# Splitting the low halves of weights and mixed values into pieces of 256 columns on GpSimd

## The chip, the cores and the metric

The kernel runs on one core of a Trainium2 chip. The metric is the device time of one execution, in microseconds (us). Several engines work side by side on a core: TensorE (PE; its weight loads are shown apart as PEld), VectorE (DVE), ScalarE (ACT), GpSimd (POOL) and SyncE (SP, which here issues the DMAs). Each works through its own queue in the order in which the program was written, and waits for the others by semaphores.

## The reference

It is a decoder of two layers over 512 positions with a width of 1024, all in 32-bit floats. In each layer a normed stream is projected once, and five groups of four heads read that projection; the groups' outputs are concatenated and projected back, and a gated MLP with a short causal convolution follows.

```
for l in range(DEPTH):                       # 2 layers
    xn = _rms_norm(x, attn_norm[l])
    h = xn @ w_in[l]
    ...                                      # per group: norm, rotary, softmax attention
    o_a = _dense_causal_attention(q_a, k_a, v_a, ...)          # "mla", low-rank q, k, v
    o_b = _dense_causal_attention(q_b, k_b, v_b, ..., decay)   # "fox", with a forgetting bias
    o_c = _moba_attention(q_c, k_c, v_c, ...)                  # "moba"
    o_d = _diff_causal_attention(q1, q2, k1, k2, v_d, lam, ...)  # "diff", two softmaxes
    o_d = _rms_norm(o_d, diff_sub_norm[l]) * (1.0 - lam_init)
    o_e = _memory_attention(q_e, k_e, v_e, ...)                # "mem", over 256 memory rows
    mixed = jnp.concatenate([_merge(o) for o in (o_a, o_b, o_c, o_d, o_e)], axis=-1)
    x = x + mixed @ w_o[l]
    xn = _rms_norm(x, ffn_norm[l])
    gate = _causal_dwconv(xn @ ffn_w_gate[l], ffn_conv_w[l], ffn_conv_b[l])
    x = x + (jax.nn.silu(gate) * (xn @ ffn_w_up[l])) @ ffn_w_down[l]
```

## The kernel before

**Products in two halves.** To keep the precision of 32-bit products, an operand is split into a high half h (a rounded copy, written as the type fp32r) and a low half l = value - h. A product of two such operands is three matmuls: h by h, h by l and l by h. Splitting is work of the other engines: for each weight ScalarE writes the high half (L419) and a subtraction gives the low half (L421). The same pair of operations splits the mixed values, the outputs of an attention pair, ahead of the output projection: L874 and L876 for most groups, L912 and L914 for the differential group. In the MLP the gated activation is split in L1625 and L1627.

**Weights.** An object of the class `Weight` stands for one load of up to 768 columns by 128 rows. It takes a staging buffer `ws` (there are 2), SP issues the load, then it takes one of 6 buffers `wh` and one of 6 `wl`, ScalarE and the subtraction fill them, and `ws` goes free for the next load. Matmuls that use a weight are planned after its `loaded` event. A layer's weights have 768, 712, 512 or 256 columns.

**The order of the work.** The kernel's code is a set of tasks, written as Python generators, and a planner in the file (`Flow`) lets them run against an estimated clock. A task yields either an event, a buffer that it needs, or a request for an engine with an estimated duration; requests that can go to one of several engines are a tuple of offers. When the planner starts an operation, the instruction is issued, so that the order in each engine's queue is the order that the planner found. An offer's estimated end is the start plus a weighted duration plus an extra:

```
    def begin(self, f, port=False):
        t = max(self.engine[f], self.now)
        return max(t, self.port) if port or f == "P" else t

    def finish(self, f, c, extra=0.0, port=False):

        return self.begin(f, port) + c * self.WEIGHT[f] + extra
```

The weights are 1.5 for VectorE ("V") and 0.6 for GpSimd ("P"). The estimate for n columns on VectorE is `both(n)` = 68 + 1.04 n ns, and on GpSimd `gps(n)` = 150 + 2.1 n ns; `vp(n)` offers both. `port` models a port that GpSimd's operations and those of VectorE marked True use one at a time. For a weight, VectorE's offer has an extra of `dear`, 400 ns, or 0 for the first layer's first weights.

**The stages.** A layer's attention part goes through the five groups in pairs of heads, in an order written out by hand (`ORDER`): projection, head norms and rotary (`rope`, L633 to L635; `rstd`, L502 and L504), scores (L763, L795), softmax (`soft`, L641 and L646), in the differential group the combination of two softmaxes (L801, L803) and the splitting of its heads (L334, L1429, with transposes in L1437), transposes (L653), the product with the values (L847, L855), and the mixed values. Output projections are accumulated into x by L974. The MLP then runs in two halves of 11 blocks of 128 columns: `ff` (L1603 to L1627) and `down` (L1675, L1696).

Of the kernel before, what the change touches and what calls it, by code (L numbers as in the profile page):

```python
# [13 lines left out]
OP = mybir.AluOpType  # L14
# [14 lines left out]
NPAIR = 2  # L29
HALF_F = NF // 2  # L30
BLK = 6

# [28 lines left out]
def mm4(n):  # L63
    return "T", 4 + max(214.0, 1.667 * n)
# [7 lines left out]
def tr(n):  # L72
    return "T", 109.0 * n - 70.0


def vec(n):
    return "V", 68 + 1.04 * n
# [11 lines left out]
def act(n):  # L89
    return "A", 94 + 0.833 * n  # L90


def both(n):

    return "V", 68 + 1.04 * n, 0.0, True


def gps(n):
    return "P", 150 + 2.1 * n
# [10 lines left out]
def dma(nbytes):  # L110
    return "D", nbytes / 330.0
# [20 lines left out]
class Flow:  # L132
# [39 lines left out]
    def free(self, tag, n=1):  # L172
        for _ in range(n):
            self.at(max(self.now, self.cur.end) + 60.0, self.freed, tag)
# [118 lines left out]
def trunk(ctx: ExitStack, tc: tile.TileContext, x_in, mem, pos, norms, sm, lam, cols, conv,  # L293
          win_mla, win_pair, win_mem, mkv, uq, ukv, w_o, gu, w_down, out):
    nc = tc.nc
    V, A, P, T = nc.vector, nc.scalar, nc.gpsimd, nc.tensor
    ENG = {"V": V, "P": P}
# [11 lines left out]
    def sbt(shape, tag, dtype=F32):  # L309
        return sb.tile(shape, dtype, name=tag + "_t", tag=tag, bufs=SLOTS[tag])  # L310

    def bank(tag):
        return ps.tile([128, 512], F32, name=tag + "_p", tag=tag, bufs=SLOTS[tag])

    def f32(ap):
        return ap.bitcast(F32)
# [4 lines left out]
    def tables(name):  # L321
        if loaded_set[0] != name:
            loaded_set[0] = name
            A.preload_act_table_set(name)
            S_.engine["A"] += 1283.0
            S_.cur.end += 1283.0
# [12 lines left out]
    def vp(n):  # L339
        return (both(n), gps(n))  # L340
# [57 lines left out]
    class Weight:  # L398
# [6 lines left out]
        def load(self):  # L405
            n = self.n
            yield self.tks[0]
            stg = sbt([128, 768], "ws")
            dst = stg[:, :n]
            if len(self.shape) == 2:  # L410
                dst = dst.rearrange("p (a b) -> p a b", a=self.shape[0])
            yield dma(512 * n)
            nc.sync.dma_start(dst, self.src)
            yield self.tks[1]
            yield self.tks[2]
            self.h = sbt([128, 768], "wh", F32R)
            self.l = sbt([128, 768], "wl", F32R)
            yield act(n)
            A.activation(self.h[:, :n], stg[:, :n], AF.Copy)  # L419
            e = yield (("V", 68 + 1.04 * n, self.dear, True), gps(n))  # L420
            ENG[e].tensor_tensor(out=self.l[:, :n], in0=stg[:, :n], in1=f32(self.h[:, :n]), op=OP.subtract)  # L421
            free("ws")

        def done(self):
# [235 lines left out]
    class Pair:  # L660
# [156 lines left out]
        def close(self, heads):  # L817
            kind, p = self.kind, self.p
            yield heads[0]
            yield heads[1]  # L820
            yield self.mx.open
            yield "V", 75.0, 0.0, True
            V.reciprocal(self.su[:, 8:16], self.su[:, 0:8])
            yield "e"
            o = sbt([128, 512], "e")
            yield act(512)
            A.activation(o.rearrange("p (k d) -> p k d", d=64), self.su[:, 8:16, None].to_broadcast([128, 8, 64]),
                         AF.Copy)
            free("st", 2 if kind == "diff" else 1)
            yield "tp"  # L830
            tp = bank("tp")
            yield tr(4)
            for i in range(NT):
                T.transpose(tp[:, 128 * i:128 * i + 128], o[:, 128 * i:128 * i + 128], ident)  # L834
            yield act(512)
            A.activation(o, tp, AF.Copy)
            free("tp")
            yield "o"
            ob = bank("o")

            for j in range(2 if kind == "mem" else NT):
                n = 512 if kind == "mem" else 512 - 128 * j
                yield "T", 4 + max(214.0, 1.667 * n) + 20
                for a in range(2):
                    pt, h = self.pt[a], slice(64 * a, 64 * a + 64)
                    if kind == "mem":
                        T.matmul(ob[h, :], self.extra.vt[:, 2 * p + j, h], pt[:, :, 128 * j:128 * j + 128],  # L847
                                 start=j == 0, stop=j == 1)
                    else:
                        if j == 3:  # L850
                            mv = pt[:, 1536:1664]
                        else:
                            mv = pt[:, 384 * j:1536].rearrange("p (i c) -> p i c", c=384)
                            mv = mv[:, :, 128 * j:128 * j + 128]
                        T.matmul(ob[h, 128 * j:512], self.src.vt[:, j, h], mv, start=j == 0, stop=j == 3)  # L855
            free("pt", 2)
            self.src.uses -= 1
            if not self.src.uses:
                if kind == "mem":
                    free("kt")  # L860
                    free("v")
                    free("qk")
                else:
                    free("v")
                    free("qk", len(self.src.qk))
            yield vec(512)
            V.tensor_tensor(out=o, in0=ob, in1=o, op=OP.mult)
            free("o")
            if kind == "diff":
                yield from self.sub_norm(o)  # L870
                return
            dst = self.mx.tile[:, p]
            yield act(512)
            A.activation(dst[:, 0, :], o, AF.Copy)  # L874
            e = yield vp(512)
            ENG[e].tensor_tensor(out=dst[:, 1, :], in0=o, in1=f32(dst[:, 0, :]), op=OP.subtract)  # L876
            free("e")

        def sub_norm(self, o):
            yield self.tk_n  # L880
            w = sbt([128, 3, 512], "pt")
            sq, y, t = w[:, 0, :], w[:, 1, :], w[:, 2, :]
            yield "A", 52 + 0.833 * 512
            A.activation(sq, o, AF.Square)
            yield "s"
            sm_ = bank("s")
            yield mm4(512)
            T.matmul(sm_, blk, sq, start=True, stop=True)
            yield "V", 65 + 1.04 * 512
            V.tensor_scalar(sq, sm_, 1.0 / 64, EPS, op0=OP.mult, op1=OP.add)  # L890
            free("s")
            yield "A", 520.0
            tables(EXP_LN)
            A.activation(y, sq, AF.Ln)
            yield "A", 520.0
            tables(EXP_LN)
            A.activation(y, y, AF.Exp, scale=-0.5)
            g = yield (("A", 52 + 0.833 * 512), both(512))
            if g == "A":
                A.activation(t, y, AF.Square)  # L900
            else:
                V.tensor_tensor(out=t, in0=y, in1=y, op=OP.mult)
            yield "V", 130 + 1.04 * 512, 0.0, True
            V.scalar_tensor_tensor(t, t, -0.5, sq, op0=OP.mult, op1=OP.mult)
            yield "V", 130 + 1.04 * 512, 0.0, True
            V.scalar_tensor_tensor(y, t, 1.5, y, op0=OP.add, op1=OP.mult)
            yield "V", 130 + 1.04 * 512, 0.0, True
            V.scalar_tensor_tensor(t, o, self.extra.sg, y, op0=OP.mult, op1=OP.mult)
            free("e")
            dst = self.mx.tile[:, self.p]  # L910
            yield act(512)
            A.activation(dst[:, 0, :], t, AF.Copy)  # L912
            e = yield vp(512)
            ENG[e].tensor_tensor(out=dst[:, 1, :], in0=t, in1=f32(dst[:, 0, :]), op=OP.subtract)  # L914
            free("pt")


# [195 lines left out]
    def layer(l, normed, rms, wm, Ly, memkv, rot):  # L1113
# [433 lines left out]
        per = HALF_F * 16  # L1547
        nt = -(-per // BLK)

        def gu_block(f, i):  # L1550
            hf, b = divmod(16 * f + i, per)
            ti, bi = divmod(b, BLK)
            if (hf, ti) not in gtiles:
                n = min(BLK, per - BLK * ti)
                gtiles[hf, ti] = Weight(gu[l, hf * nt + ti, :, :n * 128], [n * 128], n)
# [166 lines left out]
    for item in "x0 w0 x1 w1 w2 w3 x2 x3".split():  # L1722
        t = int(item[1])
# [17 lines left out]
def layout(inp):  # L1741
# [45 lines left out]
    per = HALF_F * 16  # L1787
    nt = -(-per // BLK)
    gu = np.stack([g["ffn_w_gate"], g["ffn_w_up"]], axis=1)
    gu = gu.reshape(L, 2, KD, 128, NF, 128).transpose(0, 4, 1, 2, 3, 5).reshape(L, 2, per, 128, 128)  # L1790
    pad = np.zeros((L, 2, nt * BLK, 128, 128), np.float32)
    pad[:, :, :per] = gu
    a["gu"] = c(pad.reshape(L, 2 * nt, BLK, 128, 128).transpose(0, 1, 3, 2, 4).reshape(L, 2 * nt, 128, BLK * 128))
    a["w_down"] = c(g["ffn_w_down"])
# [24 lines left out]
```

## Time and profile before

| | |
|---|---|
| median of 3 runs | 1454.44 us (1454.09 to 1459.37) |
| profiled execution | 1452.53 us, of which the span from first to last instruction is 1450.8 us |
| TensorE busy | 1386.6 us (96%), granted clock 0.982 |
| VectorE busy | 802.0 us (55%) |
| ScalarE busy | 758.4 us (52%) |
| GpSimd busy | 605.1 us (42%) |
| DMA | 117.46 MB, 81 GB/s over the span |

In the profile a row of a group of instructions gives the line, engine and operation, the tiles written and read, the shapes and the count, then the busy time in us and the mean duration in ns, then the engine's idle time ahead of them and what ended it. A row of the chain gives the start, the length and the instruction; a row of a timeline the start, the length, the engine, the line and the operation. A row of the waits says who waited for whom, for how long in total, how often, and the longest time. Busy time is an average over stages: the attention parts stand at about 50 to 400 us and 750 to 1100 us, the MLP of the first layer at 400 to 745 us, that of the second from 1100 us to the end.

### The profile page before, as it was taken

The page shows a single profiled execution, that of the slowest core. Times are in us where ns is not written, and L with a number is a line of the kernel's source. Part 1 is how long each engine was busy: PE and PEld are TensorE (multiplying, and loading weights), DVE is VectorE, ACT ScalarE, POOL GpSimd, SP SyncE. Part 2 cuts the span into 40 slices and gives each one's busy share as a digit, 9 for nine tenths or more (in the row PEclk, how much of TensorE's full clock was granted, in tenths as well). Part 3 has the DMA queues.
Part 4 walks back from the last instruction along what each step waited for, and adds up shares of the span by engine and source line. Part 5 has one row for each costly group of instructions (what it writes and reads, how often), then busy time and mean ns, then how long its engine had stood idle before and what let it go on. Part 6 is the DMA issues. An engine that isn't in the chain of part 4 may idle for free.

```text
span 1450.8 us, 21241 instructions
## 1 busy us (share of the span) xinstructions
PE 1386.6 (96%) x7392; PEld 1172.5 (81%) x7392; DVE 802.0 (55%) x2073; ACT 758.4 (52%) x1968; POOL 605.1 (42%) x423
## 2 busy tenths in 40 slices
PE   6899989999999999999999999999989999999998
PEld 5788777876888888888888887888669888888887
DVE  7777789665654402544057877887654541145411
ACT  8678566766733322433266876756764332233321
POOL 3422133333655445654532223323244554465542
PEclk9899999999999999999999999999999999999999
DMA  5311122212333233332231211220122322343223
GB/s 179 105 47 36 30 69 67 63 55 86 117 104 95 71 98 109 115 98 71 90 103 44 56 30 49 67 75 30 59 89 79 97 81 79 102 131 98 76 80 109
DMA packets 51530, 117.46 MB, mean 81 GB/s; under 512 B 6496, under 2 KB 7648, under 8 KB 51424
## 3 DMA queue, kind: packets, MB, share of 16 engines
q1 hardware_dynamic: 51424, 116.11, 26.4%
q8 instruction: 58, 0.95, 0.3%
q14 instruction: 48, 0.39, 0.1%
HBM read 113.99 MB, written 2.10 MB: 80 GB/s over the span
## 4 chain that ended last, share of the span: by engine, by line
PE 86%; DVE 7%; ACT 4%; issue 1%; DMA 0%; POOL 0%; DVEq 0%; SPq 0%; POOLq 0%; ACTq 0%
PE acc_p L479 32%; PE s_p L479 9%; PE o_p L479 8%; PE tp_p L479 8%; PE acc_p L1675 6%; PE tp_p L1675 4%; PE s_p L1675 4%; PE tp_p L653 3%; PE o_p L855 2%; PE o_p L1675 2%; PE s_p L763 2%; PE tp_p L513 1%; PE tp_p L1437 1%; DVE e_t L803 1%; PE tp_p L834 1%
## 5 line engine op out<-in xcount | busy, mean ns | idle before, releaser
L421 POOL TENSOR_TENSOR wl_t<-ws_t,wh_t 128x768 fp32r<-128x768 f32 (+3 forms) x322 | 517.2, 1612 | 624.7 <-ACT wh_t L419 568.1
L419 ACT ACTIVATE wh_t<-ws_t 128x768 fp32r<-128x768 f32 (+3 forms) x322 | 240.5, 750 | 408.2 <-DMA ws_t<-in_w_down_dram 73.2
L479 PE MATMUL acc_p<-wh_t,xh 128*128 128x384 f32 (+2 forms) x512 | 184.7, 361 | 0.4 <-DVE qn_t L933 0.4
L479 PE MATMUL acc_p<-wh_t,xl 128*128 128x384 f32 (+2 forms) x512 | 170.2, 332 | 0.0
L479 PE MATMUL acc_p<-wl_t,xh 128*128 128x384 f32 (+2 forms) x512 | 170.0, 332 | 0.0
L1608 DVE SCALAR_TENSOR_TENSOR e_t<-e_t,convt 128x511 f32<-128x511 f32 x44 | 67.6, 1536 | 172.1 <-ACT e_t L1606 172.1
L479 PE MATMUL acc_p<-wh_t,mx_t 128*128 128x512 f32 x320 | 118.6, 423 | 4.9 <-DVE x L974 2.7
L646 ACT ACTIVATE e_t<-e_t,st_t 128x256 f32<-128x256 f32 (+3 forms) x192 | 104.9, 548 | 30.0 <-DVE st_t L641 29.1
L479 PEld LDWEIGHTS acc_p<-wh_t,xh 128*128 128x128 f32 x512 | 99.0, 193 | 4.2 <-issue 1.9
L479 PEld LDWEIGHTS acc_p<-wl_t,xh 128*128 128x128 f32 x512 | 98.9, 193 | 1.0 <-issue 0.2
L479 PEld LDWEIGHTS acc_p<-wh_t,xl 128*128 128x128 f32 x512 | 98.3, 192 | 0.0
L641 DVE CUSTOM_DVE_ANT_0 e_t<-s_p,mask 128x256 f32<-128x256 f32 (+3 forms) x160 | 72.8, 473 | 23.3 <-PE s_p L763 10.0
L1618 DVE TENSOR_TENSOR e_t<-e_t 128x512 f32<-128x512 f32 x44 | 67.0, 1522 | 26.8 <-ACT e_t L1613 25.4
L479 PEld LDWEIGHTS acc_p<-wh_t,mx_t 128*128 128x128 f32 x320 | 63.5, 199 | 20.0 <-DVE x L974 3.3
L332 ACT ACTIVATE pt_t<-tp_p 128x256 f32<-128x256 f32 (+3 forms) x137 | 58.0, 432 | 35.4 <-PE tp_p L653 33.6
L653 PE MATMUL tp_p<-identr,e_t 128*128 128x128 f32 x384 | 68.2, 279 | 8.4 <-DVE e_t L803 7.7
L479 PE MATMUL acc_p<-xh,wh_t 128*128 128x512 f32 (+1 forms) x192 | 72.1, 375 | 0.0
L479 PE MATMUL acc_p<-xl,wh_t 128*128 128x512 f32 (+1 forms) x192 | 71.5, 372 | 0.0
L479 PE MATMUL s_p<-xh,wh_t 128*128 128x512 f32 (+1 forms) x192 | 71.4, 372 | 0.0
L479 PE MATMUL acc_p<-xh,wl_t 128*128 128x512 f32 (+1 forms) x192 | 71.4, 372 | 0.0
L479 PE MATMUL o_p<-xh,wh_t 128*128 128x512 f32 (+1 forms) x192 | 71.3, 371 | 0.0
L479 PE MATMUL o_p<-xl,wh_t 128*128 128x512 f32 (+1 forms) x192 | 71.3, 371 | 0.0
(265 smaller groups left out, 3321.8 us busy)
## 6 DMA issues: line engine op xcount, KB each, us to landing
ws_t<-in_gu_dram SPq DMA_DIRECT2D x116, 384.0 KB, 3.0
ws_t<-in_w_down_dram SPq DMA_DIRECT2D x88, 256.0 KB, 2.6
ws_t<-in_win_pair_dram SPq DMA_DIRECT2D x48, 384.0 KB, 3.2
ws_t<-in_w_o_dram SPq DMA_DIRECT2D x40, 256.0 KB, 2.6
ws_t<-in_mkv_dram SPq DMA_DIRECT2D x8, 384.0 KB, 3.2
ws_t<-in_win_mla_dram SPq DMA_DIRECT2D x8, 356.0 KB, 3.4
x<-in_x_dram SPq DMA_DIRECT2D x8, 256.0 KB, 4.9
pt_t<-in_mem_dram SPq DMA_DIRECT2D x4, 512.0 KB, 5.3
```

The source lines that it names most:

```text
L332: A.activation(out, in_, AF.Copy)
L419: A.activation(self.h[:, :n], stg[:, :n], AF.Copy)
L421: ENG[e].tensor_tensor(out=self.l[:, :n], in0=stg[:, :n], in1=f32(self.h[:, :n]), op=OP.subtract)
L479: T.matmul(dst, lt, rh, start=first and i == 0, stop=last and i == n - 1)
L641: V.tensor_tensor_reduce(out=e[:, :n], in0=sbank[:, :n], in1=bias, scale=-scale, scalar=BIG, op0=OP.add, op1=OP.min, accum_out=m)
L646: A.activation(e[:, :n], e[:, :n], AF.Exp, bias=m, scale=-1.0, accum_out=su)
L653: T.transpose(tp[:, j * 128:(j + 1) * 128], e[:, j * 128:(j + 1) * 128], ident)
L763: T.matmul(sbs[a][:, :n], lt, rh, start=j == 0, stop=j == 2)
L855: T.matmul(ob[h, 128 * j:512], self.src.vt[:, j, h], mv, start=j == 0, stop=j == 3)
L1608: V.scalar_tensor_tensor(c[:, 1:], b[:, :S - 1], convt[:, f, 1:2], c[:, 1:], op0=OP.mult, op1=OP.add)
L1618: V.tensor_tensor(out=c, in0=c, in1=b, op=OP.mult)
L1675: T.matmul(dbs[t][h], lt, (w.h, w.l)[wi][:, :512], start=fi == 0 and lt is gh and wi == 0, stop=fi == HALF_F - 1 and lt is gl)
```

## The change

The subtraction that gives a low half is issued in pieces of 256 columns. Each piece is a request of its own to the planner, with the estimates for its own width, so that each can be placed by itself and other operations can be planned between two pieces. It is done at three places: the weights (all of them, in the class `Weight`), and the mixed values of L876 and L914. For the weights the extra on VectorE's offer is divided by 3. A weight of 768 columns has three pieces, one of 712 has two of 256 and one of 200, one of 512 has two, one of 256 has one; a mixed value of 512 columns has two. The high halves, the MLP's activations (L1627) and all else stay as they are.

```
+PIECE = 256
...
             A.activation(self.h[:, :n], stg[:, :n], AF.Copy)
-            e = yield (("V", 68 + 1.04 * n, self.dear, True), gps(n))
-            ENG[e].tensor_tensor(out=self.l[:, :n], in0=stg[:, :n], in1=f32(self.h[:, :n]), op=OP.subtract)
+
+            for c in range(0, n, PIECE):
+                d = min(n, c + PIECE)
+                e = yield (("V", 68 + 1.04 * (d - c), self.dear / 3, True), gps(d - c))
+                ENG[e].tensor_tensor(out=self.l[:, c:d], in0=stg[:, c:d], in1=f32(self.h[:, c:d]), op=OP.subtract)
             free("ws")
...
             A.activation(dst[:, 0, :], o, AF.Copy)
-            e = yield vp(512)
-            ENG[e].tensor_tensor(out=dst[:, 1, :], in0=o, in1=f32(dst[:, 0, :]), op=OP.subtract)
+            for c in range(0, 512, PIECE):
+                e = yield vp(PIECE)
+                ENG[e].tensor_tensor(out=dst[:, 1, c:c + PIECE], in0=o[:, c:c + PIECE],
+                                     in1=f32(dst[:, 0, c:c + PIECE]), op=OP.subtract)
             free("e")
...
             A.activation(dst[:, 0, :], t, AF.Copy)
-            e = yield vp(512)
-            ENG[e].tensor_tensor(out=dst[:, 1, :], in0=t, in1=f32(dst[:, 0, :]), op=OP.subtract)
+            for c in range(0, 512, PIECE):
+                e = yield vp(PIECE)
+                ENG[e].tensor_tensor(out=dst[:, 1, c:c + PIECE], in0=t[:, c:c + PIECE],
+                                     in1=f32(dst[:, 0, c:c + PIECE]), op=OP.subtract)
             free("pt")
```

## The prediction

> **What bounds the kernel now.** I read the page first: busy time by engine, then the chain that ended last.
>
> ```profile
> PE 1386.6 (96%) x7392; PEld 1172.5 (81%) x7392; DVE 802.0 (55%) x2073; ACT 758.4 (52%) x1968; POOL 605.1 (42%) x423
> ...
> PE 86%; DVE 7%; ACT 4%; issue 1%; DMA 0%; POOL 0%; DVEq 0%; SPq 0%; POOLq 0%; ACTq 0%
> ```
>
> TensorE (PE) is busy 96% of 1450.8 us, so all that any edit of the other engines can win is its 64.2 us of idle time. POOL, which the edit loads, has 0% of the chain; DVE has 7%, about 100 us. Next I asked where PE is idle: the table by windows (PE, PEld, DVE, ACT, POOL busy, then clock).
>
> ```profile
> 0.00:50.00 50.00, 32.77 (x168) 30.00 (x169) 35.77 (x145) 38.94 (x133) 18.61 (x38) 0.88 0.48 151
> ...
> 150.00:250.00 100.00, 90.25 (x534) 78.16 (x533) 84.80 (x246) 63.77 (x191) 28.54 (x18) 0.97 0.20 58
> ...
> 400.00:700.00 300.00, 300.00 (x1356) 249.78 (x1355) 118.29 (x114) 101.60 (x147) 161.24 (x104) 1.00 0.31 94
> ...
> 850.00:1050.00 200.00, 190.37 (x1150) 158.39 (x1149) 151.66 (x455) 133.72 (x397) 61.99 (x42) 0.97 0.19 56
> ```
>
> In the MLP stage (400 to 700) PE never rests, though POOL is at its busiest there, 161 of 300 us: nothing done to POOL or DVE in that stage can win time, and PE runs on weights prepared ahead. The idle time is 17.2 us in the first 50, and 9.75 and 9.63 us in the attention windows, where the differential attention stands and where DVE is busy 85% and 76%. There the waits of PE name DVE (first 150 to 250, then 850 to 1050):
>
> ```profile
> PE tp_p L1437 <- DVE sk_t L1429: 5.3, 2, 2.7
> PE tp_p L653 <- DVE e_t L803: 4.0, 2, 2.8
> ```
>
> ```profile
> PE tp_p L653 <- DVE e_t L803: 3.7, 3, 2.2
> ...
> PE tp_p L1437 <- DVE sk_t L1429: 1.8, 2, 1.4
> PE tp_p L1413 <- DVE qn_t L635: 0.9, 2, 0.7
> ```
>
> That is 15.7 us of PE waiting for three DVE lines. Why those lines are late is in the chain, in order of time (start, length, what):
>
> ```profile
> 169.93 1.26 DVE sq_t L633
> 171.19 1.27 DVE sq_t L634
> ...
> 180.81 0.35 DVE e_t L803
> ...
> 181.35 1.84 DVE sq_t L634
> ...
> 194.21 0.23 DVE st_t L801
> ...
> 194.47 2.08 DVE e_t L803
> ...
> 218.20 1.89 DVE qn_t L635
> ...
> 228.30 0.18 DVE sq_t L633
> 228.48 0.19 DVE sq_t L634
> ...
> 228.70 0.23 DVE qn_t L635
> ...
> 229.03 1.30 DVE st_t L801
> ...
> 230.36 1.32 DVE e_t L803
> ```
>
> The same small operations take 0.18 to 0.35 us at some places and 1.26 to 2.08 us at others. What makes them long is seen in a timeline, first POOL, then DVE:
>
> ```profile
> 585.96 1.30 POOL L1627 TENSOR_TENSOR qk_t<-e_t,qk_t 128x512 fp32r<-128x512 f32 x1
> 587.20 2.31 POOL L421 TENSOR_TENSOR wl_t<-ws_t,wh_t 128x768 fp32r<-128x768 f32 x1
> ```
>
> ```profile
> 586.07 1.74 DVE L1608 SCALAR_TENSOR_TENSOR e_t<-e_t,convt 128x511 f32<-128x511 f32 x1 [2.69 <-ACT e_t L1606]
> 587.85 2.21 DVE L1610 SCALAR_TENSOR_TENSOR e_t<-e_t,convt 128x510 f32<-128x510 f32 x1
> ```
>
> The DVE operation that starts at 586.07, with POOL already at work, ends at 587.81, 0.55 us after POOL's; POOL's next one, already queued, takes 2.31 us, some 0.45 us over its usual time (next fence); the next DVE operation then lasts until 590.06, again 0.55 us after POOL. So the two engines exclude each other on such operations, and a waiting DVE operation comes in between two queued POOL operations. Its wait is at most what is left of one POOL operation, and the change cuts just that.
>
> **The change part by part.** POOL's operations by shape (count, busy us, mean ns):
>
> ```profile
> L421 POOL TENSOR_TENSOR wl_t<-ws_t,wh_t 128x768 fp32r<-128x768 f32 x176 | 327.5, 1865 | 367.1 <-ACT wh_t L419 322.6 <-ACT st_t L498 24.4 <-PE s_p L795 6.5
> L421 POOL TENSOR_TENSOR wl_t<-ws_t,wh_t 128x512 fp32r<-128x512 f32 x134 | 173.3, 1298 | 228.1 <-ACT wh_t L419 216.1 <-PE acc_p L479 7.2 <-ACT st_t L498 2.5
> ...
> L876 POOL TENSOR_TENSOR mx_t<-e_t,mx_t 128x512 fp32r<-128x512 f32 x16 | 21.0, 1310 | 111.0 <-ACT mx_t L874 111.0
> ...
> L421 POOL TENSOR_TENSOR wl_t<-ws_t,wh_t 128x712 fp32r<-128x712 f32 x8 | 13.6, 1712 | 23.5 <-ACT wh_t L419 23.5
> L914 POOL TENSOR_TENSOR mx_t<-pt_t,mx_t 128x512 fp32r<-128x512 f32 x4 | 5.1, 1280 | 41.6 <-ACT mx_t L912 34.4 <-PE s_p L795 7.2
> L421 POOL TENSOR_TENSOR wl_t<-ws_t,wh_t 128x256 fp32r<-128x256 f32 x4 | 3.0, 742 | 6.0 <-ACT wh_t L419 6.0
> ```
>
> *Which engine.* 176 + 134 + 8 + 4 = 322: every weight residual is on POOL, as are all 20 of the mixed values. In the planner DVE's offer for such an operation never starts before POOL's (both wait for the shared port) and its weighted cost is higher at 768 columns and at 256 (1.5 x 334 + 133 = 634 against 0.6 x 688 = 413), so I take all pieces to stay on POOL.
>
> *POOL's own time.* The 256-column row gives a piece directly: 742 ns. A 768-column weight becomes 2.226 us (+0.361), a 512-column one 1.484 (+0.186), a 712-column one 2.10 (+0.39, its last 200 columns at 0.618 by the slope of the rows), a mixed value 1.484 (+0.174 or +0.204). Sum: 176 x 0.361 + 134 x 0.186 + 8 x 0.39 + 16 x 0.174 + 4 x 0.204 = 95 us in 522 more instructions. Queued operations overlap a little (585.96 + 1.30 = 587.26 against a start at 587.20), some 0.04 to 0.06 us each, so it may be 70. POOL goes from 605 to 675 to 700 us, under half of the span.
>
> The row price of one more instruction is thus 0.18 us. [...]
>
> *What hides it.* Each weight is prepared in the background behind six buffers of each half; no wait of PE for a weight residual stands among PE's waits, so +0.36 us per weight costs nothing as long as that lead holds. Behind POOL stand the staging buffer, and so SP's next weight load, and what else SP has queued behind that. Pieces of two weights, or of a weight and a mixed value, can alternate in the new order, which ends the first later by up to two pieces, 1.4 us. If the lead is gone somewhere, that is the price there.
>
> *Where it isn't hidden: the start.* POOL and SP in the first 20 us:
>
> ```profile
> 8.54 1.69 POOL L421 TENSOR_TENSOR wl_t<-ws_t,wh_t 128x712 fp32r<-128x712 f32 x1 [5.46 <-ACT wh_t L419]
> 15.79 3.39 POOL L421 TENSOR_TENSOR wl_t<-ws_t,wh_t 128x712 fp32r<-128x712 f32 x2 [5.56 <-ACT wh_t L419]
> ```
>
> ```profile
> 10.26 0.33 SPq L413 DMA_DIRECT2D ws_t<-in_win_mla_dram  x1
> ...
> 17.53 0.33 SPq L413 DMA_DIRECT2D ws_t<-in_win_mla_dram  x1
> ```
>
> The third load goes out 0.03 us after POOL's first residual ends, the fourth likewise. Two residuals in line, each 0.3 us longer with the overlap: +0.6 us taken; between 0 (the first matmuls wait for x instead) and 1.2 (four in line).
>
> *The mixed value ahead of the output projection.* It is on the chain once in each layer:
>
> ```profile
> 350.42 1.29 POOL mx_t L876
> ```
>
> Two pieces with their overlap are 1.44 us: +0.13 to 0.15 in each layer, up to +0.85 if a weight's piece comes between. Both layers: 0.3 to 1.7; taken 0.6, one such piece in about one of two layers.
>
> *What is won.* In 150 to 250 the seven long rows above exceed their short forms (0.18, 0.19, 0.23, 0.23, 0.35) by 1.08 + 1.08 + 1.65 + 1.73 + 1.66 + 1.07 + 0.97 = 9.2 us. In 850 to 1050 the chain has 13 such rows of 1.15 us and more, 18.9 us together; first and last:
>
> ```profile
> 856.91 1.15 DVE st_t L504
> ...
> 1017.92 1.36 DVE qn_t L635
> ```
>
> By the same kind of short forms their excess is some 15.4 us. So 20 waits of 1.23 us on the chain. With pieces the rest of one POOL operation is at most 0.74 us and, met at random, half of it: a wait of 0.37 to 0.70 remains, 43 to 70% goes. Of PE's 15.7 us that is 6.8 to 11.0 us. Something else is late next: PE also waits for the out-projection's addition (L974) and for the maxima (L641), and a chain of DVE operations that came through together after one long wait may now meet two pieces. I take 5.5 us, nearer the low end for that reason.
>
> *Sum.* 0.6 + 0.6 - 5.5 = -4.3 us. The profiled execution took 1452.5 us, with 1.7 us around its span, and stands 1.9 us under the median of the runs shown, 1454.4. So 1452.5 - 4.3 + 1.9 = 1450 us.
>
> **The rivals.** *All of the wait reaches PE (faster).* The waits fall by 70%, 11.0 us, and nothing comes next, with the small costs at 0.6: 1454.4 - 10.4 = 1444 us. For it: in 150 to 250 the two waits for DVE are 9.3 of PE's 9.75 us idle, and the clock there is 0.97. Against it: PE is idle less than the chain's DVE waits add up to (19.4 us against 24.6), so it has other work for some of them.
>
> *The pieces meet more operations (slower).* Three pieces give three chances to stop DVE where there was one. Rows at 169.93 and 171.19 show two neighbours that each waited for a POOL operation. If a former wait of 1.23 us becomes two and a half of 0.70, 1.75 us, the 20 waits cost 10.4 us more, and with the 1.2 us of the start and the mixed values the time is 1454.4 + 10.4 + 1.2 = 1466. It decides from the point where a weight's three pieces stop on average more than 1.8 DVE operations (1.23 / 0.70). Against it: POOL is busy only 31% of 850 to 1050, and many DVE operations read PSUM or one input and don't wait.
>
> *The change doesn't let DVE in.* If POOL's next piece kept the port, a weight would hold it for 2.14 us in place of 1.87, and 20 waits would grow by 0.27: 5.4 us, half of it on PE, plus 1.2: 1458 us. [...] The rows at 586 to 590 speak against that reading: the queued POOL operation was the one that waited.
>
> **How the numbers follow.** Half a per cent is 7.3 us, about what a measurement of this kernel can tell from no change. Small gain, 1448 to 1454: 0.40; no letting in, 1458: 0.05; faster rival, under 1447: 0.35; slower rival, over 1461.7: 0.20. The planner also lays out every queue anew, which no row prices; an attention window's idle time, 9.7 us, is my scale for what it can add or remove, and it widens all cases. Faster 0.35, same 0.45, slower 0.20. Range 1440 to 1463: below it lies the top of the gain with a lucky order, above it the slower rival's full price.
>
> **What would show it.** Right: L421 in some 820 pieces on POOL, mean near 735 ns, POOL near 690 us; hardly a DVE row of L633 to L635, L801, L803 over 1.1 us; PE's waits for L1429 and L803 in the attention windows down by about half; 400 to 700 still full. Wrong: pieces on DVE; PE waiting for wl_t; DVE busy time in the attention windows as before or higher; a PE idle of over 64 us at other places than now, which would be the new order's doing.

## The result, and the profile after

The changed kernel takes 1430.1 us (median of 4 runs, 1426.5 to 1434.9) against 1454.3 us; the ratio is 0.983, with a 95% interval of 0.980 to 0.986. It is 24 us faster, where 4 us had been forecast. The profiled executions stand 26.1 us apart in their spans, 1450.8 and 1424.7 us. (Line numbers after are 4 to 8 higher: L425 is the weights' residual, L637 to L639 the rotary, L807 the combination of the two softmaxes, L1437 the splitting of its heads, L881 and L921 the mixed values.)

The page of the changed kernel, busy time and the chain:

```profile
PE 1371.5 (96%) x7392; PEld 1159.7 (81%) x7392; DVE 739.3 (52%) x2062; ACT 759.4 (53%) x1979; POOL 713.3 (50%) x945
...
PE 84%; DVE 6%; ACT 5%; DMA 2%; POOL 2%; issue 1%; SPq 0%; DVEq 0%; ACTq 0%; POOLq 0%
```

DVE lost 62.7 us of busy time with nearly the same work (11 of its 2073 operations went to ACT): most of that is waiting that the record counts as busy, as the kernel with the old order shows below, which has all 2073 and loses 68 us. POOL gained 108 us. PE, which does exactly the same 7392 matmuls, is busy 15.1 us less, and idle 53.2 us in place of 64.2. So 11.0 us of the 26.1 are idle time, and 15.1 are the same matmuls in less time. The table by windows shows both (the last figure before the DMA columns is the granted clock):

```profile
0.00:50.00 50.00, 36.50 (x232) 33.75 (x233) 35.32 (x161) 44.12 (x150) 21.90 (x57) 1.00 0.51 166
...
150.00:250.00 100.00, 97.47 (x606) 85.04 (x606) 83.26 (x253) 71.66 (x217) 40.61 (x54) 1.00 0.24 69
...
400.00:700.00 300.00, 300.00 (x1326) 248.39 (x1325) 94.59 (x109) 100.15 (x147) 196.34 (x240) 1.00 0.30 95
...
850.00:1050.00 200.00, 194.52 (x1179) 162.04 (x1177) 148.26 (x453) 141.11 (x413) 77.65 (x107) 1.00 0.19 59
```

In the two attention windows the idle time falls from 19.4 to 8.0 us, and the clock rises from 0.97 to 1.00. In the first 50 us the clock rises from 0.88 to 1.00. The windows are fixed in time, and the changed kernel is further on in them. Not all that lies between gained: from 250 to 400 us the idle time rose from 5.2 to 9.2 us (first row before, second after), and the end of the first attention part, around 350 us, has become the changed kernel's longest stretch at a low clock, with PE waiting 6.9 us for DVE's L527, which prepares the stream for the MLP (third row, after):

```profile
250.00:400.00 150.00, 144.77 (x936) 121.40 (x934) 99.44 (x304) 105.78 (x304) 60.37 (x41) 0.99 0.25 78
```

```profile
250.00:400.00 150.00, 140.84 (x896) 118.20 (x895) 91.12 (x267) 97.25 (x271) 66.83 (x90) 0.95 0.24 75
...
340.00:362.00 22.00, 13.83 (x72) 11.26 (x71) 14.51 (x49) 17.17 (x61) 6.95 (x10) 0.69 0.23 66
```

PE's waits in 150 to 250, where the waits for the two lines of DVE that stand below had made 9.3 us before:

```profile
PE tp_p L657 <- DVE e_t L807: 0.4, 2, 0.2
PE tp_p L1445 <- DVE sk_t L1437: 0.3, 1, 0.3
```

The pieces on POOL, by shape:

```profile
L425 POOL TENSOR_TENSOR wl_t<-ws_t,wh_t 128x256 fp32r<-128x256 f32 x816 | 619.9, 785 | 609.0 <-ACT wh_t L420 514.6 <-issue 71.9 <-PE s_p L799 6.9
...
L881 POOL TENSOR_TENSOR mx_t<-e_t,mx_t 128x256 fp32r<-128x256 f32 x32 | 23.1, 737 | 42.5 <-ACT mx_t L878 42.5
...
L425 POOL TENSOR_TENSOR wl_t<-ws_t,wh_t 128x200 fp32r<-128x200 f32 x8 | 4.9, 614 | 0.0
```

All are on POOL. The median piece of a weight takes 737 ns, close to the old 256-column row (742 ns); the mean of 785 ns has waiting for DVE on top. That DVE comes in between two pieces is seen around 187 us, first POOL, then DVE:

```profile
187.18 0.78 POOL L425 TENSOR_TENSOR wl_t<-ws_t,wh_t 128x256 fp32r<-128x256 f32 x1 [2.74 <-ACT wh_t L420]
...
187.92 1.05 POOL L425 TENSOR_TENSOR wl_t<-ws_t,wh_t 128x256 fp32r<-128x256 f32 x1
```

```profile
187.38 0.99 DVE L807 SCALAR_TENSOR_TENSOR e_t<-e_t,st_t 128x384 f32<-128x384 f32 x1
```

DVE's operation, begun during the first piece, ends 0.41 us after it, and the second piece, already queued, takes 1.05 us in place of 0.74. Of the 232 operations of the rotary and of the combination (L633 to L635, L801, L803) 20 took over 1.1 us before, up to 2.07; after, none does.

**The clock behind a pause.** In the trace of before, one of the pauses that the prediction counted, with what comes after it:

```profile
222.00:229.00 7.00, 7.00 (x38) 5.71 (x36) 6.76 (x21) 5.78 (x16) 0.00 (x0) 1.00 0.23 63
229.00:231.80 2.80, 0.02 (x1) 0.00 (x1) 2.73 (x3) 0.85 (x3) 2.75 (x3) 1.00 0.00 0
232.20:235.60 3.40, 3.06 (x8) 2.48 (x9) 1.92 (x6) 0.98 (x5) 1.17 (x1) 0.50 0.71 176
236.00:240.00 4.00, 4.00 (x25) 3.41 (x24) 3.28 (x13) 1.65 (x5) 0.00 (x0) 1.00 0.04 14
```

PE works until 229.0 at full clock, pauses for 2.8 us, and then runs for 3.4 us at half the clock, doing 8 matmuls where the next 4 us have 25 (of the 512-column ones in a row one starts every 0.43 us, from 236 us on every 0.23). This pause is paid twice. Not every one is: a pause of 2.7 us in the same trace is followed by full clock:

```profile
182.60:185.30 2.70, 0.04 (x1) 0.00 (x0) 2.67 (x4) 0.00 (x0) 2.25 (x2) 1.00 0.42 99
185.60:189.00 3.40, 3.40 (x21) 2.96 (x21) 3.33 (x12) 1.90 (x7) 0.00 (x0) 1.00 0.48 125
```

Over the whole span the mean clock tells the sum:

```profile
core 0: 1450.8 us, clock 0.982
```

```profile
core 0: 1424.7 us, clock 0.993
```

Before (first) 1.8% of 1450.8 us is 26.1 us lost to the clock, after (second) 0.7% of 1424.7 us is 10.0 us. The difference of 16.1 us is about the 15.1 us by which PE is less busy. The changed kernel's own four executions, one program, say the same: at clocks of 0.993, 0.990, 0.988 and 0.985 the spans were 1424.7, 1427.5, 1429.1 and 1433.1 us. The kernel before, in 13 executions of a later experiment, ranges from 1449.4 us at 0.985 to 1459.0 us at 0.978. So the span goes with the clock even where program and order are the same. The profiled execution of the changed kernel is the best of its four; at the median some 10 of the 24 us are the clock's (an estimate: a clock of 0.989 over 1428.3 us loses 15.7 us, against the 26.1 of before).

Half the clock for 3.4 us is what this trace shows behind the pause of 2.8 us, and not behind the one of 2.7 us.

### The profile page after: what moved, and what is told of

The parts are those of the page before. It is cut to its first block, busy times and chain, and to the rows that moved or that the text cites. A ratio compares the mean times of both kernels' runs of the same rounds, so it can differ in the third digit from the quotient of the medians.

```text
span 1424.7 us, 21833 instructions
## 1 busy us (share of the span) xinstructions
PE 1371.5 (96%) x7392; PEld 1159.7 (81%) x7392; DVE 739.3 (52%) x2062; ACT 759.4 (53%) x1979; POOL 713.3 (50%) x945
## 4 chain that ended last, share of the span: by engine, by line
PE 84%; DVE 6%; ACT 5%; DMA 2%; POOL 2%; issue 1%; SPq 0%; DVEq 0%; ACTq 0%; POOLq 0%
PE acc_p L483 32%; PE s_p L483 9%; PE tp_p L483 8%; PE o_p L483 8%; PE acc_p L1683 5%; PE tp_p L1683 3%; PE s_p L1683 3%; PE tp_p L657 3%; PE o_p L859 2%; PE s_p L767 2%; POOL wl_t L425 2%; PE o_p L1683 2%; DMA ws_t<-in_w_down_dram 2%; ACT wh_t L420 1%; ACT xh L523 1%
## 5 line engine op out<-in xcount | busy, mean ns | idle before, releaser
L425 POOL TENSOR_TENSOR wl_t<-ws_t,wh_t 128x256 fp32r<-128x256 f32 x824 | 624.4, 783 | 609.0 <-ACT wh_t L420 514.6
L483 PE MATMUL acc_p<-wh_t,xh 128*128 128x384 f32 (+2 forms) x512 | 181.5, 354 | 5.4 <-DVE st_t L508 2.1
L1616 DVE SCALAR_TENSOR_TENSOR e_t<-e_t,convt 128x511 f32<-128x511 f32 x44 | 54.4, 1236 | 178.5 <-ACT e_t L1614 178.5
L483 PE MATMUL acc_p<-wh_t,mx_t 128*128 128x512 f32 x320 | 113.7, 406 | 2.2 <-DVE qn_t L941 1.3
L650 ACT ACTIVATE e_t<-e_t,st_t 128x384 f32<-128x384 f32 (+3 forms) x192 | 104.6, 546 | 15.8 <-DVE st_t L645 15.3
L483 PEld LDWEIGHTS acc_p<-wh_t,mx_t 128*128 128x128 f32 x320 | 60.3, 188 | 15.5 <-DVE qn_t L941 1.4
L483 PE MATMUL tp_p<-xh,wh_t 128*128 128x512 f32 (+1 forms) x192 | 71.4, 372 | 0.0
L483 PE MATMUL o_p<-xh,wl_t 128*128 128x512 f32 (+1 forms) x192 | 71.3, 371 | 0.0
L483 PE MATMUL tp_p<-xh,wl_t 128*128 128x512 f32 (+1 forms) x192 | 71.3, 371 | 0.0
```

Of the source, the lines that this page charges most:

```text
L425: ENG[e].tensor_tensor(out=self.l[:, c:d], in0=stg[:, c:d], in1=f32(self.h[:, c:d]), op=OP.subtract)
L483: T.matmul(dst, lt, rh, start=first and i == 0, stop=last and i == n - 1)
L650: A.activation(e[:, :n], e[:, :n], AF.Exp, bias=m, scale=-1.0, accum_out=su)
L1616: V.scalar_tensor_tensor(c[:, 1:], b[:, :S - 1], convt[:, f, 1:2], c[:, 1:], op0=OP.mult, op1=OP.add)
```

## The experiments

**Pieces or order?** The change does two things: it cuts the instructions, and it lets the planner lay out every queue anew. Two kernels do one each. The first plans as before and cuts at issue (the mixed values alike):

```
+            e = yield (("V", 68 + 1.04 * n, self.dear, True), gps(n))
+            for c in range(0, n, 256):
+                d = min(n, c + 256)
+                ENG[e].tensor_tensor(out=self.l[:, c:d], in0=stg[:, c:d], in1=f32(self.h[:, c:d]), op=OP.subtract)
```

> The order of before in every queue, planned with whole operations; only the instruction is cut in pieces of 256 when it is issued. Theory A (the pieces themselves win: VectorE gets in between them, whatever the order): most of the 26 us, 1430 to 1440 us, and the excess of two-input VectorE operations under GpSimd falls as it did in the changed kernel (from about 137 to 70 us over the whole span). Theory B (the new order wins, which the planner lays out because it is told of short GpSimd operations): about as before, 1449 to 1456 us, though the waits of VectorE get shorter. GpSimd near 700 us busy in both.

Measured: 1436.2 us, ratio 0.988 (0.986 to 0.989). Its page and two windows:

```profile
PE 1382.4 (96%) x7392; PEld 1170.3 (82%) x7392; DVE 734.0 (51%) x2073; ACT 759.0 (53%) x1968; POOL 712.1 (50%) x945
```

```profile
150.00:250.00 100.00, 94.64 (x567) 82.30 (x566) 82.59 (x255) 67.78 (x200) 35.84 (x48) 0.97 0.20 58
...
850.00:1050.00 200.00, 194.96 (x1178) 161.66 (x1177) 145.33 (x456) 136.59 (x401) 73.30 (x102) 0.99 0.19 58
```

The same order in every queue, 107 us more busy time on POOL, and 16.6 us less in the span (1434.2): 12.4 of idle time, 4.2 of PE's busy time. In the two windows the idle time is 10.4 us in place of 19.4.

The second plans with pieces, as the changed kernel does, and issues one whole instruction where the last piece would stand:

```
             for c in range(0, n, PIECE):
                 d = min(n, c + PIECE)
                 e = yield (("V", 68 + 1.04 * (d - c), self.dear / 3, True), gps(d - c))
-                ENG[e].tensor_tensor(out=self.l[:, c:d], in0=stg[:, c:d], in1=f32(self.h[:, c:d]), op=OP.subtract)
+            ENG[e].tensor_tensor(out=self.l[:, :n], in0=stg[:, :n], in1=f32(self.h[:, :n]), op=OP.subtract)
```

> The order of the changed kernel in every queue, planned with pieces; but one whole GpSimd instruction is issued at the place of the last piece. Theory A: no gain or a loss, 1450 to 1462 us, with waits of VectorE of up to 1.9 us back. Theory B: 1428 to 1438 us. If the gain is half and half, both this and the kernel with the old order lie near 1440 us.

Measured: 1460.6 us, ratio 1.0045 (1.0029 to 1.0061), slower than before, with long VectorE operations again (this row was 1522 ns before and is 793 in the changed kernel):

```profile
L1624 DVE TENSOR_TENSOR e_t<-e_t 128x512 f32<-128x512 f32 x44 | 62.7, 1425 | 18.8 <-ACT e_t L1619 16.5
```

So the gain is the pieces': 17 us in the old order and 30 us in the new one. The new order with whole operations loses 6 to 8 us; planned for short operations, it pays only with them, and then adds some 6 us. (The loss is not the order's alone: the whole subtraction stands where the last piece would, later than the plan has its first piece.) Theory A holds, theory B for the small rest.

**Which operations?** Pieces planned and issued for one kind alone (the other kind's lines as before):

> Pieces for the weights alone, planned and issued; the 20 mixed values whole. Theory A: nearly all of the gain, as 318 of the 338 operations that are cut are weights: 1428 to 1436 us. Theory B: anything between 1425 and 1450 us, since each change of a plan gives another order.

Measured: 1433.8 us, ratio 0.987 (0.985 to 0.989).

> Pieces for the 20 mixed values alone; weights whole. Theory A: as before within 0.3%, 1450 to 1458 us, since 20 short waits at most are touched. Theory B: a new order too, so it can differ from before by as much as the changed kernel does, on either side; a gain of over 10 us here would speak for the order alone.

Measured: 1445.3 us, ratio 0.994 (0.991 to 0.996). The weights carry most of it, as theory A says. The mixed values win more than it allowed; with 20 operations cut and a new order at once, this run does not tell which of the two it was.

Then the weights by stage. In the old order, pieces for the MLP's weights alone (an argument of the class, 256 for the gate, up and down weights and 768 for the others):

> Old order, pieces of 256 for the MLP's weights alone (gate, up and down), all else whole. Theory A with TensorE full in the MLP stage: 1450 to 1454 us, a gain of 3 us at most at the stage's ends. If shorter VectorE operations in the MLP win time of their own: 1440 to 1448 us.

Measured: 1451.2 us, ratio 0.997 (0.995 to 0.999): some 4 us, as small as PE's full MLP stage had let one expect. The other side, the changed kernel with the MLP's weights whole:

> The changed kernel, but the MLP's weights whole, planned and issued. By theory A the gain lies in the attention stages and TensorE is full in the MLP: 1428 to 1438 us, as the changed kernel (1430) or up to the 4 us later that pieces in the MLP alone had won in the old order. If alternating pieces cost something at the MLP's ends in the changed kernel too: 1422 to 1428 us.

Measured: 1432.9 us, ratio 0.984 (0.982 to 0.986), no different from the changed kernel. The gain lies in the attention stages.

**Is it GpSimd's reading?** In the old order, three memsets of zeros in place of each weight's subtraction; the low halves of the weights are left out:

```
-            ENG[e].tensor_tensor(out=self.l[:, :n], in0=stg[:, :n], in1=f32(self.h[:, :n]), op=OP.subtract)
+            for m in (n, n, n // 2):
+                P.memset(f32(self.l[:, :m]), 0.0)
```

> Old order, but GpSimd's weight residuals are replaced by three memsets of zeros of about the same total length, so the low halves of the weights are left out (zero) and GpSimd reads nothing for a weight. If two-input VectorE operations are held up by GpSimd's reads, hardly any of them should be long beside a memset, and the time shows what all such waits cost together. Theory A: 1428 to 1436 us, at or a few us below the old order in pieces (1436). If the waits have another cause than the shared reading: 1448 us or more.

Measured: 1422.3 us, ratio 0.975 (0.972 to 0.979). VectorE's and GpSimd's rows:

```profile
L1609 DVE SCALAR_TENSOR_TENSOR e_t<-e_t,convt 128x511 f32<-128x511 f32 x44 | 33.1, 751 | 177.9 <-ACT e_t L1607 177.9
...
L1619 DVE TENSOR_TENSOR e_t<-e_t 128x512 f32<-128x512 f32 x44 | 30.4, 692 | 54.7 <-ACT e_t L1614 53.5
```

```profile
L422 POOL MEMSET wl_t<- 128x768 f32 x352 | 261.3, 742 | 288.2 <-PE acc_p L480 178.7 <-PE tp_p L480 48.6 <-PE s_p L480 18.2
```

The first row was 1536 ns before, the second 1522. POOL is as busy as before (617 against 605 us), but for the weights it only writes, and these long VectorE operations are gone. The time is 33 us shorter (the kernel before took 1455.5 us beside it). That is a rough price of being held up by the weights' residuals in this order, since something else changes too: a memset waits neither for the load nor for ScalarE's high half, so the low halves are ready earlier. Of the cause the two runs show this: with subtractions, which read two tiles, the first row took 1536 ns on average, with memsets, which only write, 751.

**How short?** The old order, cut at 128 columns:

> Old order, instructions cut in pieces of 128 columns. Theory A (wait in proportion to the piece): the excess of two-input VectorE operations under GpSimd falls again by a third to a half, and the time to 1430 to 1436 us, unless GpSimd's own fixed cost (about 0.18 us in each of some 1690 pieces, 850 to 870 us busy in all) makes weights late: then 1438 to 1450 us, and TensorE waits for wl_t.

Measured: 1432.8 us, ratio 0.983 (0.980 to 0.986). The excess of VectorE's operations under POOL, each over the median of the same operation with POOL idle (left out: the convolution's first one, which has no undisturbed case), goes 102, 50, 35 us from whole operations to 256 and 128 columns, and the time 1454, 1436, 1433. A piece of 128 columns takes 0.46 to 0.50 us, more than half of 742 ns, and POOL was busy 854 us. Even so PE waited for `wl_t` only once, for 0.4 us:

```profile
L424 POOL TENSOR_TENSOR wl_t<-ws_t,wh_t 128x128 fp32r<-128x128 f32 x1640 | 755.0, 496 | 409.9 <-ACT wh_t L420 352.1 <-issue 52.3 <-PE acc_p L482 3.4
...
L880 POOL TENSOR_TENSOR mx_t<-e_t,mx_t 128x128 fp32r<-128x128 f32 x64 | 28.2, 471 | 99.6 <-ACT mx_t L877 99.5
```

Cutting each piece in two in the changed kernel's order:

> The changed kernel's order, each piece issued as two of 128 columns. In the old order the step from 256 to 128 columns went from 1436 to 1433 us. Theory A: as much here, 1425 to 1430 us, by shorter waits again. If GpSimd, some 850 us busy, is late with weights in this order: 1432 to 1445 us, with TensorE waiting for wl_t.

Measured: 1436.3 us, ratio 0.988 (0.985 to 0.991), so not better than the changed kernel, and probably worse. PE does wait for wl_t, but briefly:

```profile
PE acc_p L1687 <- POOL wl_t L427: 1.5, 2, 1.0
...
PE tp_p L1687 <- POOL wl_t L427: 0.4, 1, 0.4
```

That is less than the distance of 6 us; the rest stays open. Part of it is in the clock: in the profiled pair, 1435.3 and 1424.7 us, PE's busy time makes 8.3 of 10.6 us. And planned at 128 columns as well:

> Planned and issued in pieces of 128 columns. Theory A gives 1422 to 1432 us, the planner's order for short pieces and the shortest waits together; but the planner counts 419 ns for such a piece, 2.5 us for a weight of 768 columns, and may hold weights back: then 1432 to 1450 us.

Measured: 1534.9 us, ratio 1.055 (1.052 to 1.059): 80 us slower. PE's waits, the chain, and the MLP's window:

```profile
PE acc_p L1683 <- POOL wl_t L425: 20.0, 13, 2.8
PE tp_p L1683 <- POOL wl_t L425: 19.2, 11, 3.0
```

```profile
PE 47%; POOL 20%; DMA 16%; ACT 8%; DVE 5%; issue 3%; ACTq 0%; SPq 0%; POOLq 0%; DVEq 0%
```

```profile
400.00:700.00 300.00, 282.53 (x1195) 225.43 (x1194) 80.74 (x108) 91.80 (x132) 214.97 (x409) 0.97 0.28 85
```

POOL has room (215 of 300 us), but weights are late. POOL's pieces and SP's weight loads in a stretch of that stage show why:

```profile
565.66 0.86 POOL L425 TENSOR_TENSOR wl_t<-ws_t,wh_t 128x128 fp32r<-128x128 f32 x2 [2.62 <-ACT wh_t L420]
566.95 2.51 POOL L425 TENSOR_TENSOR wl_t<-ws_t,wh_t 128x128 fp32r<-128x128 f32 x6 [0.42 <-ACT wh_t L420]
```

```profile
562.24 1.16 SPq L414 DMA_DIRECT2D ws_t<-in_w_down_dram  x2
568.66 1.16 SPq L414 DMA_DIRECT2D ws_t<-in_gu_dram  x2
```

POOL does two pieces of a weight that has four, then waits for the high half of another weight: in this plan the pieces of two weights alternate. Both staging buffers come free together, the loads go out in twos, over 6 us apart, and load and residual no longer overlap. The short pieces alone are not the reason: the kernel with the old order, cut at 128 columns, has as many of them in that stage, weight after weight, and PE is full:

```profile
400.00:700.00 300.00, 300.00 (x1326) 248.39 (x1325) 83.56 (x111) 100.43 (x146) 233.49 (x453) 1.00 0.31 94
```

The test, with the MLP's weights whole and everything else planned at 128:

> Planned and issued in pieces of 128 columns, but the MLP's weights (gate, up, down) whole. Theory D (the kernel planned with 128 columns throughout lost 80 us because pieces of two weights alternate, both staging buffers come free together and the MLP's loads go out in twos): the MLP stage is full again and no wait for wl_t is left there; 1425 to 1440 us. Rival (the planner's order for pieces of 128 is bad in the attention stage itself): over 1480 us.

Measured: 1431.3 us, ratio 0.983 (0.980 to 0.986), and the MLP stage is full:

```profile
400.00:700.00 300.00, 300.00 (x1325) 248.43 (x1324) 117.16 (x111) 101.54 (x148) 161.90 (x106) 1.00 0.30 95
```

Theory D holds: the loss was the MLP's weight supply, in the order of the pieces and not in their length. The changed kernel plans in pieces there too, and its chain had begun to touch DMA and POOL (2% each); at 256 columns the lead still covers it.

**The MLP's activations too.** The changed kernel with the third such subtraction (L1635) in pieces:

> The changed kernel with the MLP's activations also split in pieces of 256. TensorE is full in that stage, so by theory A nothing is to be won there, 1426 to 1434 us; a gain or loss of over 5 us would have to come from another order at the stage's ends.

Measured: 1432.1 us, ratio 0.985 (0.982 to 0.988): nothing, as expected.

**What does a pause cost?** Extra matmuls in the kernel before, ahead of seven places with transposes for which PE had waited; they shorten no wait of VectorE. First 92 of 128 columns:

```
+        fill("e", tp, nj)      # at seven places: tp[:, 0:128] = identr x identr, 7 to 18 times
         for j in range(nj):
             T.transpose(tp[:, j * 128:(j + 1) * 128], e[:, j * 128:(j + 1) * 128], ident)
```

> The kernel before, whole operations and old order, with 92 small extra matmuls on TensorE, issued into banks that are overwritten next, ahead of seven transposes of the differential group for which TensorE had waited 1.2 to 2.8 us. They shorten no wait of VectorE; they only keep TensorE at work in the pause. Theory C (each pause costs a second time, because the granted clock falls to half for 3.4 us or more after it): the half-clock stretches after these pauses, 17 us in all at 174, 232, 894 and 952 us, go, and with them up to 8.5 us: 1443 to 1449 us against 1453. Rival (a low clock after a pause costs nothing, since TensorE waits there anyway): 1451 to 1457 us, the stretches gone or not.

Measured: 1451.8 us, ratio 0.997 (0.995 to 0.999), mean clock 0.982 as before. The small matmuls filled most of each pause and did not hold the clock: behind the pause shown above, filled with 18 of them (2.12 of its 2.8 us), a 512-column matmul still starts 0.43 us after the one before it (233.47 and 233.90 us). So this run says nothing on its price; its gain of 0.3% stays unexplained. Then 11 large ones (ident x mask, 512 columns, 32 bits):

> As the kernel with the 92 small fillers, but each pause is filled with one or two matmuls of 512 columns in 32 bits (11 in all), since the small ones left the granted clock as it was. Theory C (a pause costs again by the half clock behind it): if TensorE's work in the pause now holds the clock, the half-clock time falls from 53 us to under 40 us and the span by up to 8 us, to 1443 to 1449 us. Rival (a low clock there costs nothing): 1451 to 1457 us though the half-clock time falls. If the half-clock time stays at 50 us or more, the run says nothing on the price.

Measured: 1446.8 us, ratio 0.995 (0.993 to 0.997), mean clock 0.988 in place of 0.982. The pause shown above, in this kernel:

```profile
219.00:226.00 7.00, 7.00 (x36) 5.64 (x36) 6.79 (x22) 5.79 (x17) 0.41 (x1) 1.00 0.29 87
226.00:228.80 2.80, 2.33 (x10) 1.02 (x8) 2.70 (x6) 1.44 (x4) 2.18 (x2) 1.00 0.03 6
229.20:232.60 3.40, 2.80 (x12) 2.22 (x13) 3.19 (x10) 1.26 (x5) 1.75 (x1) 1.00 0.56 134
```

The stretch behind it runs at full clock, 12 matmuls in place of 8. VectorE is held up as much as before (799 us busy against 802), and PE does work that nobody needs, yet the span is 5.8 us shorter. So the half clock behind a pause costs time by itself, as theory C has it and as the executions of one program at different clocks, above, let one expect. The size is rough: the mean clock says that 17.3 us were lost to it in place of 26.1, of which the span kept 5.8, some half-clock stretches at other places moved too, and the interval of this kernel overlaps that of the small matmuls.

None of these kernels beats the changed one beyond its interval, apart from the one that leaves the low halves out.

## Why the prediction was wrong, and where it was right

Right were the mechanism and where it acts: POOL and DVE exclude each other on such operations (0.99 us in place of the 0.62 without POOL for DVE's combination at 187 us), a waiting DVE operation comes in between two queued pieces (1.05 us in place of 0.74 for the second), PE's waits for the splitting of heads and for the combination shrink in the attention windows, and the MLP stage can't win. Right was that all pieces stay on POOL, at a price of about 742 ns (the median is 737). POOL's busy time grew by more than the forecast 70 to 95 us, by 108, because a piece that lets DVE in is longer by that wait; it cost nothing. The rival in which DVE is not let in is excluded by the kernel with the old order (1436 us against its 1458) and by the rows at 187 us, and the one in which pieces meet more operations by DVE's 68 us less of busy time in the old order.

Wrong was the size of the term "What is won", 5.5 us, and with it the range, at three places:

- *The clock was left out.* The prediction named 0.97 in two windows and priced nothing by it, and it took PE's 64.2 us of idle time for all that could be won. A pause was counted once, and many are paid twice: some 52 us of the span of before stand at half clock (double the 26.1 us lost). In the profiled pair PE's busy time is 15.1 of the 26.1 us; at the median some 10 of 24 us are the clock's, and in the profiled pair of the old order only 4.2 of 16.6.
- *The discount for "something else is late next".* The bracket for the waits named was 6.8 to 11.0 us, and 5.5, which lies below it, was taken as "nearer the low end". In the old order the two windows lost 9.0 us of idle time, well inside the bracket: there, nothing else came next that took the gain back. The 5.5 was a guess without a row. In the new order something did come next, outside these windows: the 4 us of idle time added between 250 and 400 us.
- *The waits outside the two windows.* Only the two attention windows were counted. In the old order another 3.4 us of idle time went elsewhere. The start, forecast at +0.6 us, was a gain: 36.5 us of matmuls in the first 50 us in place of 32.8, in the profiled execution at full clock. The +0.6 us for the mixed values did not fall due: in the old order PE's wait for POOL's mixed value at the end of the first attention part is 0.5 us, before it was 0.7.

The new order, left unpriced but for a scale of 9.7 us, added some 6 us on top of the old order's 17. No row had priced it, so that it fell on the side of the gain was luck. The price named for lost cover, pieces of two weights that alternate, did not fall due at 256 columns; at 128 it cost 80 us.

The faster rival (1444 us, 0.35) had the right sign, and its 11.0 us are close to the idle time that went (11.0 in the changed kernel, 12.4 in the old order). It was still 14 us too slow, most of that for want of the clock.

## What to carry to other kernels

Where two engines exclude each other on an operation, its length is the other's longest wait (here up to 1.69 us over the undisturbed time beside subtractions of up to 768 columns, 1.85 us, and up to 0.61 us beside pieces of 0.74); cut the long operations of the engine that has time, even at a fixed price for each piece, and look for the gain only in stages where the matmul engine waits. Price a pause of TensorE with the half clock that can follow it (here 3.4 us behind a pause of 2.8): add up (1 - granted clock) times the span beside the idle time, as the most that the clock can give back. When a planner sees the pieces too, check that pieces of two loads don't alternate, since two staging buffers that come free together are no double buffer (here the loads then went out in twos, over 6 us apart, and the kernel lost 80 us).

## What the runs showed of the hardware

- A pause of TensorE of 2.8 us was followed by 3.4 us at half clock, another of 2.7 us was not. 18 matmuls of 128 columns in the place of the first did not prevent it (behind them a 512-column matmul started 0.43 us after the one before it, at full clock 0.23); with two of 512 columns in 32 bits the stretch behind had full clock (one execution of each).
- A GpSimd subtraction of 128, 256, 512 and 768 columns took 0.47 (the mixed values), 0.74, 1.29 and 1.85 us: some 0.18 us for the instruction and 2.2 ns for a column, an estimate from these four.
- With GpSimd memsets of the same tiles in place of the subtractions, a two-input VectorE operation of 128x511 took 751 ns on average, in place of 1536.
- VectorE's addition that reads PSUM (L974, 128x512) took 686 ns beside a GpSimd subtraction and 686 without, a reduce of 128x256 with one input (L927) 413 and 418 (medians, the kernel before). A cast of 128x256, also with one input, did wait: 1.39 us beside a subtraction (L334 at 168.54 us), 0.29 without.
- A VectorE operation that waited during one GpSimd subtraction went ahead of the next one, though that was already queued (187 us: the second took 1.05 us in place of 0.74).
